# A hybrid decoder layer on one core: a new order of the opening, new places for gate and up's outputs, and the last tiles of W_o by halves in turn

## The chip, the cores and the metric

The kernel runs on one core of one Trainium2 chip. The metric is the device time of one execution in microseconds (us). The profile shows one execution, taken by the hardware profiler. Engines are named as the profile names them: PE is TensorE's matrix multiplication and PEld its loading of weights, DVE is VectorE, ACT is ScalarE, POOL is GpSimd, SP is SyncE, which only issues DMA transfers. "SPq" and "POOLq" mark what an engine's sequencer does.

## The reference

One layer of a decoder (width 1024) over a prompt of 2048 tokens and, beside it, over 8 decode tokens that come with a window of keys and values and with a state. All arrays are float32. What is computed, cut to its core:

```python
def finish(x, o_attn, o_gla, r_gla, gla_norm_g, w_o, ffn_norm_g, w_gate, w_up, w_down):
    ...
    h = x + jnp.concatenate([o_attn.astype(x.dtype), g], axis=-1) @ w_o
    z = rmsnorm(h, ffn_norm_g)
    return h + (jax.nn.silu(z @ w_gate) * (z @ w_up)) @ w_down

def reference(...):
    ...
    q_a, k_a, v_a, q_g, k_g, v_g, r_g, log_a = project(rmsnorm(xp, attn_norm_g[l]), *proj_w)
    o_a = prompt_window_attention(q_a, k_a, v_a, rel_bias, attn_sinks[l])
    ...
    o_g, s_p = gla_chunked(q_g, k_g, v_g, log_a, s0)
    xp = finish(xp, o_a, o_g, r_g, *ffn_w)
```

`project` is one product with `w_in` (1024 x 2320), followed by norms of each head. The attention is a sliding window of 128 keys with sinks and a relative bias; group B is gated linear attention (GLA). D_FF is 2816. For the decode tokens the window of keys and values moves on by one: 127 rows of each cache go to the outputs `k_win_sample` and `v_win_sample` as they are, and the new row behind them.

## The kernel before

**Precision.** Each float32 operand is split into a high and a low part (`split`, line 96: ScalarE casts the high part, VectorE subtracts it), and each product is three matmuls (`mm3`, line 107; lines 109 to 111 of the profile): high by high, high by low, low by high. So nearly each operand costs one instruction on ACT and one on DVE (lines 97 and 98 of the profile) before PE can use it.

**Order.** The tile framework orders the instructions of each engine with a planner that runs a simulated timeline over the whole program. The program's text sets priorities, not the order: an instruction without dependencies, such as a load, may be put far ahead of where it stands. `tc.issue_after(ins)` binds the instructions of a block that run on `ins`'s engine to come after `ins` in that engine's order. Nearly all DMA transfers are issued by SP in one order; an issue that waits holds up those behind it. Some are issued by POOL, on its own queue.

**Stage A (lines 149 to 596): projection and attention, block by block of 128 tokens.** `front(b)` loads a block of x, normalises it, transposes it on PE (line 144) and splits it. `project(b)` multiplies it with WA (q, k, v and the low-rank gate's columns, 784 wide), `project_r(b)` with WR (512 wide), `attend(b)` computes the attention and stores it in `mix_d[b]`. WA and WR are loaded and split once, at the opening, by `staged_split` (line 178); every second call of it, if the piece is large enough, takes the piece as one load of 1024 columns, the others in loads of 512. `make_bias` (line 523) multiplies a one-hot table with the bias table on PE (line 538), stores the result (`ext`) in DRAM (line 541), loads it back shifted for each row (`rev`, line 548) and flips it on PE (line 550) into `bias`, which `attend` needs. `nTdec` is a zeroed tile (line 85) which the decode tokens' `norm_T` fills later. The decode tokens' part of the stage is a generator that is advanced once in each block. At b == 3 stands a block (lines 581 to 592) with loads for the next stage (gg, w2, bT) and two copies from cache to output inside DRAM.

**Stage B (lines 628 to 1000)** is the gated linear attention; it adds to `mix_d`.

**Stage M (lines 1077 to 1225): W_o, residual, norm, and the operands of gate and up.** The 16 tiles of 128 tokens, and then the 8 decode tokens as tile NB, go through `load_tile`, `product` (two halves `dh` of W_o's columns, 24 matmuls each at 512 columns, or 16 for the decode tokens) and `after`, which calls `normalise` for the tile before and, for every second tile, `operands`. gate and up are computed with Strassen's scheme in the form with seven products: `operands` forms the seven sums of z's four quarters (b11, b21, b12, b22), splits them and stores them in `zc_d` by POOL's queue. Three buffers (`hlp`) hold what is being stored; the last four of the last tile go into the memory of the two `mix` tiles.

**Gate and up (lines 1283 to 1366).** The tokens go in two halves `sb` of 1024, and for each half in 11 pairs `fp` of weight columns. `pair` runs the seven products in the order P1, P6, P2, P7, P5, P4, P3 for gate and up. Each product needs one z operand in SBUF (`zc`, 2 MB each, loaded at line 1361) and one split weight unit (`whl`). P1 is copied out of PSUM by ACT into `p1` (line 1256), and P2 goes on accumulating in the same bank. The outputs of the products live in 14 tiles of 516 columns (`out`, line 1231), two for each of seven names.

**Memory.** The SBUF is filled from both ends. Stage M's tiles on the right lie, from the highest address down, as: z operands 0 and 1, W_o's two halves, the two mix tiles, three store buffers, gBf with z, and lowest b0 to b3 with zd. In gate and up, z operands 2 and 3 take the place of W_o's first half, 4 and 5 that of the second half, 6 that of the mix tiles, and the 14 output tiles lie over the rest, lowest first in the order in which their names first occur within a pool. So each of these loads and first writes waits until the last reader of what lay there is done.

**Down (lines 1370 to 1475)** multiplies with w_down in the same scheme and adds to h; it uses the same `out` tiles.

Of the kernel before, what the change touches and what calls it, by code (L numbers as in the profile page):

```python
# [53 lines left out]
def hymba_kernel(ctx: ExitStack, tc: tile.TileContext, I, O, X=None, phases=3):  # L54
# [94 lines left out]
    with ExitStack() as ph:  # L149
# [15 lines left out]

        gB = early.tile([P, D], F32, name="gB")
# [9 lines left out]
        staged = [0]  # L176
# [16 lines left out]
        def load_wq(k, nk):  # L193
            staged_split(WA[:, 0, k:k + nk, 0:512], WA[:, 1, k:k + nk, 0:512], w_in[:, k:k + nk, 0:512], 512)

        def load_wkv(k):
            staged_split(WA[:, 0, k:k + 4, 512:768], WA[:, 1, k:k + 4, 512:768], w_in[:, k:k + 4, 512:768], 256)
# [4 lines left out]
        def load_wr(k):  # L202
            staged_split(WR[:, 0, k:k + 2], WR[:, 1, k:k + 2], w_in[:, k:k + 2, 1792:2304], 512)
# [157 lines left out]
        def attend(b):  # L361
# [62 lines left out]
            nc.sync.dma_start(mix_d[b][:, 0:4, :], o.rearrange("p (c t) -> p c t", c=4))  # L424
# [98 lines left out]
        def make_bias():  # L523


            with tc.tile_pool(name="a_ext", bufs=1) as ep:
# [17 lines left out]
                nc.sync.dma_start(dbias_d[:, 0:1], ext[:, P - 1:P])  # L544

# [21 lines left out]
        project(1)  # L567
        project_r(0)
        project_r(1)
        dec = decode_a()  # L570
        for b in range(NB):
# [6 lines left out]
            attend(b)  # L578
            if b >= 1:
                next(dec, None)  # L580
            if b == 3:
                nc.sync.dma_start(gg, I["gla_norm_g"].rearrange("o d -> d o"))
                w2 = pc.tile([16, 256], F32, name="w2")
                nc.sync.dma_start(w2, I["w_gla_gate2"][0])
                split(w3[0:16], w3[64:80], w2)
                nc.vector.tensor_copy(w3[32:48], w3[0:16].bitcast(F32))
                for p in range(2):
                    nc.sync.dma_start(bT[:, p:p + 1], I["b_gla_gate"][0:1, p * P:(p + 1) * P].rearrange("o d -> d o"))
                nc.gpsimd.tensor_scalar(nbT, bT, -1.0, None, ALU.mult)
                for nm_, cache in (("k_win_sample", "cache_k"), ("v_win_sample", "cache_v")):  # L590
                    nc.sync.dma_start(O[nm_][0, :, 0:P - 1].rearrange("n t h d -> n t (h d)"),
                                      I[cache][0, :, 1:P].rearrange("n t h d -> n t (h d)"))
# [473 lines left out]

    def load_w(w, fp):
        raws = []
        for kh in range(2):
            wr = craw.tile([P, 1024], F32, tag="raw", name="wrg").rearrange("p (k n) -> p k n", k=4)  # L1070
            nc.sync.dma_start(wr, w[kh * 512:(kh + 1) * 512, fp * 256:(fp + 1) * 256].rearrange("(k p) n -> p k n", p=P))
# [5 lines left out]
    with ExitStack() as ph:  # L1077
# [6 lines left out]
        zp = pool(ph, "m_z", 1, side="right")  # L1084
        bp = pool(ph, "m_b", 1, side="right")
# [42 lines left out]
        def product(ti, mt, h):  # L1128
            n = P if ti < NB else ND
            for dh in range(2):  # L1130
# [8 lines left out]
                add_h(h, n, dh, ps)  # L1139
            if ti < NB:  # L1140
# [3 lines left out]
            return h  # L1144
# [66 lines left out]
        for i, ti in enumerate(tiles):  # L1211
# [5 lines left out]
            hs[ti] = product(ti, *now)  # L1217
            if ti < NB and i:
                after(tiles[i - 1])
# [63 lines left out]
    with ExitStack() as ph:  # L1283
# [74 lines left out]
        for sb in range(2):  # L1358
            zc = {name: ztile(q, f"z{q}") for q, name in enumerate(PRODS)}
            for q, name in enumerate(PRODS):  # L1360
                nc.sync.dma_start(zc[name][:, :, :, 0:512].bitcast(F32), zc_d[sb][q])
# [3 lines left out]
            for fp in range(NP):  # L1365
                pair(sb, fp, zc)

# [161 lines left out]
```

## Time and profile before

| | us |
|---|---|
| median of three runs | 2242.85 |
| lowest and highest of them | 2240.05, 2245.52 |
| the profiled execution | 2241.9 |
| its span, first to last instruction | 2239.8 |
| PE busy in it | 2184.7 |

The granted clock of TensorE is 0.994 on the mean of the span. The busy share of PE, the granted clock and the share of the DMA engines in 40 equal slices of 56 us, as tenths:

```profile
PE   7999998999999999899999999999999999999997
PEclk9999999999999999999999999999999999999999
DMA  7323325445535898842333376445352698779776
```

Stage A takes the first 6 or 7 slices, stage B lasts until the 13th, stage M fills slices 13 to 16, gate and up 17 to 32, down the rest. A row of a timeline reads: start in us, duration in us, engine, line, operation, tiles (written <- read), shape, count, and in brackets how long the engine sat idle before it and what ended that.

### The profile page before, as it was taken

Reading aid. Unit: us, or ns where it says so; the run is one execution under the profiler, and the core shown is the slowest. Engines: PE = TensorE matmul, PEld = TensorE weight load, DVE = VectorE, ACT = ScalarE, POOL = GpSimd, SP = SyncE. Lnnn points to the kernel's source line nnn. Section 1 sums busy time; section 2 is a strip of 40 time slices with the busy share of each in tenths; the row PEclk is TensorE's granted clock in tenths of the full one; section 3 lists DMA queues with packets and bytes.
Section 4 is the critical chain, followed back from the end, with each engine's and each line's share of the span. In section 5 each row is a group of like instructions: output and inputs, shape, how many; then the busy total and the mean of one; then the engine's idle time right before and its main releaser. Section 6 shows DMA issues by size and latency. Waiting matters only on the chain.

```text
span 2239.8 us, 34849 instructions
## 1 busy us (share of the span) xinstructions
PE 2184.7 (98%) x12573; PEld 1883.0 (84%) x12573; DVE 1579.5 (71%) x3129; ACT 982.0 (44%) x2249; POOL 686.7 (31%) x788
## 2 busy tenths in 40 slices
PE   7999998999999999899999999999999999999997
PEld 6788887888897887688888889999999978787886
DVE  7788888677866667666666667777776645657486
ACT  6656766565655344323333233334333324334342
POOL 2555665574665233111111111110111122222222
PEclk9999999999999999999999999999999999999999
DMA  7323325445535898842333376445352698779776
GB/s 228 110 77 119 119 77 183 125 152 167 175 116 199 298 350 272 316 131 82 113 95 107 105 266 216 149 127 165 101 187 86 220 285 188 184 170 243 167 195 236
DMA packets 218060, 386.35 MB, mean 172 GB/s; under 512 B 16440, under 2 KB 129872, under 8 KB 214800
## 3 DMA queue, kind: packets, MB, share of 16 engines
q1 hardware_dynamic: 180400, 279.48, 37.7%
q0 software_dynamic: 37488, 104.65, 18.1%
q8 instruction: 99, 1.62, 0.3%
q14 instruction: 73, 0.60, 0.1%
HBM read 221.84 MB, written 163.30 MB: 172 GB/s over the span
## 4 chain that ended last, share of the span: by engine, by line
PE 55%; issue 18%; DVE 10%; POOL 6%; ACT 4%; DMA 3%; SPq 0%; POOLq 0%; DVEq 0%; ACTq 0%
PE ps_b L110 5%; PE ps_b L109 5%; PE ps_b L111 5%; POOL h_d L1457 4%; PE ps_c L110 4%; PE ps_c L109 4%; PE ps_c L111 4%; PE ps_a L110 4%; PE ps_a L111 4%; PE ps_a L109 4%; PE ps_wo L111 2%; PE ps_wo L109 2%; PE ps_wo L110 2%; ACT S L394 1%; PE ps_v L109 1%
## 5 line engine op out<-in xcount | busy, mean ns | idle before, releaser
L110 PE MATMUL ps_b<-z,whl 128*128 128x258 f32 (+1 forms) x792 | 253.4, 320 | 0.0
L109 PE MATMUL ps_b<-z,whl 128*128 128x258 f32 (+1 forms) x792 | 253.0, 320 | 0.0
L111 PE MATMUL ps_b<-z,whl 128*128 128x258 f32 (+1 forms) x792 | 252.1, 318 | 0.0
L97 ACT CAST dm<-mr 128x384 fp32r<-128x384 f32 (+1 forms) x224 | 107.8, 488 | 201.9 <-PE ps_b L111 102.4
L109 PE MATMUL ps_a<-z,whl 128*128 128x258 f32 (+1 forms) x528 | 169.8, 322 | 5.1 <-ACT gp L1256 4.4
L109 PE MATMUL ps_c<-z,whl 128*128 128x258 f32 (+1 forms) x528 | 169.4, 321 | 2.1 <-DMA z<-zc_d_P 2.1
L111 PE MATMUL ps_a<-z,whl 128*128 128x258 f32 (+1 forms) x528 | 169.6, 321 | 0.5 <-DVE whl L98 0.5
L110 PE MATMUL ps_a<-z,whl 128*128 128x258 f32 (+1 forms) x528 | 169.7, 321 | 0.0
L110 PE MATMUL ps_c<-z,whl 128*128 128x258 f32 (+1 forms) x528 | 169.6, 321 | 0.0
L111 PE MATMUL ps_c<-z,whl 128*128 128x258 f32 (+1 forms) x528 | 169.5, 321 | 0.0
L98 DVE TENSOR_TENSOR dm<-mr,dm 128x384 fp32r<-128x384 f32 (+1 forms) x224 | 115.2, 519 | 64.3 <-ACT dm L97 64.1
L111 PEld LDWEIGHTS ps_b<-z,whl 128*128 128x128 f32 x792 | 148.8, 188 | 11.9
L109 PEld LDWEIGHTS ps_b<-z,whl 128*128 128x128 f32 x792 | 148.9, 188 | 11.8
L110 PEld LDWEIGHTS ps_b<-z,whl 128*128 128x128 f32 x792 | 148.8, 188 | 11.8
L97 ACT CAST whl<-wrg 128x512 fp32r<-128x512 f32 x132 | 81.6, 619 | 162.1 <-PE ps_b L111 76.8
L1356 POOL DMA_DIRECT2D md_d<-m x22 | 15.6, 710 | 356.7 <-DVE m L1315 356.7
L1023 DVE TENSOR_TENSOR gu<-ps_c,gu 128x512 f32<-128x512 f32 (+1 forms) x130 | 77.9, 599 | 53.0 <-PE ps_c L111 52.3
L98 DVE TENSOR_TENSOR whl<-wrg,whl 128x512 fp32r<-128x512 f32 x132 | 90.7, 688 | 33.8 <-ACT whl L97 33.7
L849 POOL TENSOR_TENSOR bd<-E,qTb 64x256 f32<-64x256 f32 x112 | 101.5, 906 | 41.4 <-ACT E L837 26.6
L109 PEld LDWEIGHTS ps_a<-z,whl 128*128 128x128 f32 x528 | 100.1, 190 | 13.9 <-ACT gp L1256 4.8
L97 ACT CAST whl<-sy 128x512 fp32r<-128x512 f32 x88 | 54.5, 619 | 125.0 <-PE ps_b L111 70.9
L109 PEld LDWEIGHTS ps_c<-z,whl 128*128 128x128 f32 x528 | 100.1, 190 | 10.6 <-issue 2.5
(424 smaller groups left out, 6681.0 us busy)
## 6 DMA issues: line engine op xcount, KB each, us to landing
mr<-md_d SPq DMA_DIRECT2D x24, 1344.0 KB
zc_d_P<-zhl POOLq DMA_DIRECT2D x56, 512.0 KB, 6.8
z<-zc_d_P SPq DMA_DIRECT2D x14, 2048.0 KB
wrg<-in_w_gate_dram SPq DMA_DIRECT2D x44, 512.0 KB
wrg<-in_w_up_dram SPq DMA_DIRECT2D x44, 512.0 KB
nT_d<-nT SPq DMA_DIRECT2D x16, 1024.0 KB
zT<-nT_d SPq DMA_DIRECT2D x8, 2048.0 KB
h_d<-gu POOLq DMA_DIRECT2D x48, 256.0 KB, 5.4
```

What stands on the lines that cost most here:

```text
L97: nc.scalar.copy(h, src)
L98: (eng or nc.vector).tensor_tensor(l, src, h.bitcast(F32), ALU.subtract)
L109: nc.tensor.matmul(ps, lh, rh, start=start, stop=False, skip_group_check=more)
L110: nc.tensor.matmul(ps, lh, rl, start=False, stop=False, skip_group_check=more)
L111: nc.tensor.matmul(ps, ll, rh, start=False, stop=stop, skip_group_check=more)
L394: nc.scalar.activation(St[:, c], St[:, c], AF.Exp, bias=nm[:, h:h + 1], accum_out=den[:, h:h + 1])
L849: nc.gpsimd.tensor_tensor(bv[rows, h], E5[rows, :, :, 1], qv[rows, :, :, 1], ALU.mult)
L1023: nc.vector.tensor_tensor(out, a, b, ALU.add)
L1356: nc.gpsimd.dma_start(md_d[sb][g][:, :, q, fp - GROUPS[g][0], :], src.rearrange("p (m t) -> p m t", m=4))
L1457: nc.gpsimd.dma_start(h_d[ti][:, cols], c, accum_op=ALU.add)
```

## The change

- **Opening.** 30 matmuls on the zeroed `nTdec` come first on PE, and ten transposes of tile 0 after `front(0)`, all into a PSUM tile that nobody reads. `front(1)` stands ahead of the last four of the q weights; the low-rank columns are loaded after k and v's. Which pieces come as one load is given by position. `make_bias` is a generator: its first part (to the store of `ext`) stands where it stood, its second after `project(1)`.
- **The block at b == 3.** The loads of gg, w2 and bT are bound behind the store of `attend(3)`; the two cache copies move to gate and up, behind the weight loads of the third pair of the first half.
- **Stage M.** `product` yields after each half of W_o; for the last tile (15) and the decode tokens the halves are run in turn: 15 first half, NB first half, 15 second half, NB second half, and then tile 11's `after`. A pool of 128 columns that nobody uses lies where zd made room, and zd now lies in mdec's memory.
- **Gate and up.** The 14 output tiles are placed one by one in three pools: m11, gu3, uu3 (first of each) and m11's second in the lowest; gp1, up1, gu2, uu2 (first of each) in the next; the others above. The seventh z operand of the first half is loaded by POOL's queue.

```diff
+        zeros = nTdec.rearrange("p k t -> p (k t)")
+        ps_warm = aux.tile([P, 512], F32, tag="aux", name="ps_warm")
+        for i in range(30):
+            nc.tensor.matmul(ps_warm[:, :320], zeros[:, 0:P], zeros, start=True, stop=True)
...
-        def staged_split(hi, lo, src, width):
+        def staged_split(hi, lo, src, width, whole=False):
...
-            staged[0] += 1
-            if staged[0] % 2 == 0 and nk * width > 512:
+            if whole:
...
         front(0)
+        for i in range(10):
+            nc.tensor.transpose(ps_warm[:, :P], xt0[:, 0:P], ident)
         load_wq(0, 1)
         load_wq(1, 1)
-        for k in range(2, KD, 2):
+        load_wq(2, 2)
+        front(1)
+        for k in range(4, KD, 2):
             load_wq(k, 2)
-        front(1)
-        load_lr()
         load_wkv(0)
         load_wkv(4)
+        load_lr()
         load_gains()
-        make_bias()
+        turn = make_bias()
+        next(turn)
         for k in range(0, KD, 2):
             load_wr(k)
         project(0)
         project(1)
+        next(turn, None)
         project_r(0)
...
-            attend(b)
+            stored = attend(b)
...
             if b == 3:
...
+                with tc.issue_after(stored.ins):
+                    nc.sync.dma_start(gg, I["gla_norm_g"].rearrange("o d -> d o"))
+                    nc.sync.dma_start(w2, I["w_gla_gate2"][0])
...
-                for nm_, cache in (("k_win_sample", "cache_k"), ("v_win_sample", "cache_v")):
-                    nc.sync.dma_start(O[nm_][0, :, 0:P - 1].rearrange("n t h d -> n t (h d)"),
-                                      I[cache][0, :, 1:P].rearrange("n t h d -> n t (h d)"))
...
+        pool(ph, "m_gap", 1, side="right").tile([P, 128], F32, name="gap")
         bp = pool(ph, "m_b", 1, side="right")
...
                 add_h(h, n, dh, ps)
+                yield
...
-                d = bp.tile([P, 8, 4, 4], F32, name="zd")
+                d = mdec.rearrange("p f n -> p (f n)")[:, 0:128].rearrange("p (q k t) -> p q k t", q=8, k=4)
...
-            hs[ti] = product(ti, *now)
-            if ti < NB and i:
-                after(tiles[i - 1])
+            hs[ti] = now[1]
+            if i < len(tiles) - 2:
+                for _ in product(ti, *now):
+                    pass
+                if i:
+                    after(tiles[i - 1])
+            elif ti < NB:
+                last = product(ti, *now)
+            else:
+                both = last, product(ti, *now)
+                for _ in range(3):
+                    for p in both:
+                        next(p, None)
+                after(tiles[-3])
...
-    cy1, cy2 = pool(ctx, "c_out1", 2), pool(ctx, "c_out2", 2)
+    cys = [pool(ctx, f"c_out{i}", 1) for i in range(3)]
+    PLACE = {"m110": 0, "m111": 0, "gu30": 0, "uu30": 0, "gp10": 1, "up10": 1, "gu20": 1, "uu20": 1}
+    turns = {}
 
     def out(tag, name):
-        return (cy2 if tag in ("gu3", "uu2", "uu3") else cy1).tile([P, 516], F32, tag=tag, name=name)
+        n = turns[tag] = turns.get(tag, -1) + 1
+        tag += str(n % 2)
+        return cys[PLACE.get(tag, 2)].tile([P, 516], F32, tag=tag, name=name)
...
-                nc.sync.dma_start(zc[name][:, :, :, 0:512].bitcast(F32), zc_d[sb][q])
+                (nc.gpsimd if (sb, q) == (0, 6) else nc.sync).dma_start(zc[name][:, :, :, 0:512].bitcast(F32), zc_d[sb][q])
...
                 pair(sb, fp, zc)
+                if sb == 0 and fp == 2:
+                    with tc.issue_after(loaded[0].ins):
+                        for nm_, cache in (("k_win_sample", "cache_k"), ("v_win_sample", "cache_v")):
+                            nc.sync.dma_start(O[nm_][0, :, 0:P - 1].rearrange("n t h d -> n t (h d)"),
+                                              I[cache][0, :, 1:P].rearrange("n t h d -> n t (h d)"))
```

`loaded[0]` is the last weight load that `load_w` issued.

More of the change, by code (lines that the diff above doesn't have):

```diff
@@ L174, in hymba_kernel @@
         w_in = I["w_in"][0].rearrange("(k p) n -> p k n", p=P)
-        staged = [0]
-        def staged_split(hi, lo, src, width):
+        def staged_split(hi, lo, src, width, whole=False):
             nk = src.shape[1]
-            staged[0] += 1
-            if staged[0] % 2 == 0 and nk * width > 512:
+            if whole:
                 wr = wl.tile([P, D], F32, tag="pT", name="wr", bufs=3).rearrange("p (k n) -> p k n", n=width)
@@ L193, in load_wq @@
         def load_wq(k, nk):
-            staged_split(WA[:, 0, k:k + nk, 0:512], WA[:, 1, k:k + nk, 0:512], w_in[:, k:k + nk, 0:512], 512)
+            staged_split(WA[:, 0, k:k + nk, 0:512], WA[:, 1, k:k + nk, 0:512], w_in[:, k:k + nk, 0:512], 512, k == 4)
         def load_wkv(k):
-            staged_split(WA[:, 0, k:k + 4, 512:768], WA[:, 1, k:k + 4, 512:768], w_in[:, k:k + 4, 512:768], 256)
+            staged_split(WA[:, 0, k:k + 4, 512:768], WA[:, 1, k:k + 4, 512:768], w_in[:, k:k + 4, 512:768], 256, True)
         def load_lr():
@@ L202, in load_wr @@
         def load_wr(k):
-            staged_split(WR[:, 0, k:k + 2], WR[:, 1, k:k + 2], w_in[:, k:k + 2, 1792:2304], 512)
+            staged_split(WR[:, 0, k:k + 2], WR[:, 1, k:k + 2], w_in[:, k:k + 2, 1792:2304], 512, k % 4 == 2)
         gq = pc.tile([P, 1], F32, name="gq")
@@ L423, in attend @@
                 nc.vector.tensor_tensor(o[rh], po[rh], ol[rh], ALU.add)
-            nc.sync.dma_start(mix_d[b][:, 0:4, :], o.rearrange("p (c t) -> p c t", c=4))
+            return nc.sync.dma_start(mix_d[b][:, 0:4, :], o.rearrange("p (c t) -> p c t", c=4))
         def decode_a():
@@ L581, in hymba_kernel @@
             if b == 3:
-                nc.sync.dma_start(gg, I["gla_norm_g"].rearrange("o d -> d o"))
                 w2 = pc.tile([16, 256], F32, name="w2")
[L584 to L589, printed above, removed]
-                for nm_, cache in (("k_win_sample", "cache_k"), ("v_win_sample", "cache_v")):
-                    nc.sync.dma_start(O[nm_][0, :, 0:P - 1].rearrange("n t h d -> n t (h d)"),
-                                      I[cache][0, :, 1:P].rearrange("n t h d -> n t (h d)"))
+                with tc.issue_after(stored.ins):
+                    nc.sync.dma_start(gg, I["gla_norm_g"].rearrange("o d -> d o"))
+                    nc.sync.dma_start(w2, I["w_gla_gate2"][0])
+                    split(w3[0:16], w3[64:80], w2)
+                    nc.vector.tensor_copy(w3[32:48], w3[0:16].bitcast(F32))
+                    for p in range(2):
+                        nc.sync.dma_start(bT[:, p:p + 1], I["b_gla_gate"][0:1, p * P:(p + 1) * P].rearrange("o d -> d o"))
+                    nc.gpsimd.tensor_scalar(nbT, bT, -1.0, None, ALU.mult)
         project_r(NB - 2)
@@ L1065, in sums_b @@
         yield b22
+    loaded = [None]
     def load_w(w, fp):
@@ L1070, in load_w @@
             wr = craw.tile([P, 1024], F32, tag="raw", name="wrg").rearrange("p (k n) -> p k n", k=4)
-            nc.sync.dma_start(wr, w[kh * 512:(kh + 1) * 512, fp * 256:(fp + 1) * 256].rearrange("(k p) n -> p k n", p=P))
+            loaded[0] = nc.sync.dma_start(wr, w[kh * 512:(kh + 1) * 512, fp * 256:(fp + 1) * 256].rearrange("(k p) n -> p k n", p=P))
             raws.append(wr)
@@ L1139, in product @@
                 add_h(h, n, dh, ps)
+                yield
             if ti < NB:
@@ L1143, in product @@
                 nc.gpsimd.dma_start(hdec_d, h[:n])
-            return h
         def normalise(ti, h, bs):
```

## The prediction

> **What bounds the kernel now.** I read the page's busy times first, then the waits of TensorE (PE) in the two stretches that the change touches, then the timelines of the queues there.
>
> ```profile
> PE 2184.7 (98%) x12573; PEld 1883.0 (84%) x12573; DVE 1579.5 (71%) x3129; ACT 982.0 (44%) x2249; POOL 686.7 (31%) x788
> ```
>
> TensorE is busy 2184.7 of 2239.8 us. The change takes no matmul of the computation away, so it can only win idle TensorE time (55.1 us in all) and time at the lower clock. Here are the PE waits of the first 150 us, and then those of 860 to 1000 us, where the W_o phase turns into the gate/up phase (columns: total, times, longest):
>
> ```profile
> PE ps_nT L144 <- DVE xt L139: 8.5, 2, 8.3
> PE ps_rev L550 <- DMA rev<-ext_d: 1.9, 1, 1.9
> PE ps_nT L144 <- DVE nTdec L98: 1.5, 1, 1.5
> PE ps_nT L144 <- DVE xtd L139: 1.1, 1, 1.1
> ```
>
> ```profile
> PE ps_a L109 <- ACT gp L1256: 4.4, 1, 4.4
> PE ps_c L109 <- DMA z<-zc_d_P: 2.1, 1, 2.1
> PE ps_a L109 <- ACT whl L97: 0.7, 1, 0.7
> PE ps_a L111 <- DVE whl L98: 0.5, 1, 0.5
> ```
>
> The 8.3 us are the first tile's load and norm, which the change does not shorten. What can go is the wait for rev (1.9), and the four at the turn (7.7). The waits at 91 to 97 us (1.5 and 1.1) belong to the decode tokens' norm, which is not edited.
>
> A wait costs more than itself, because the clock drops. The windows view (busy, PEclk, DMA share, GB/s) behind each wait:
>
> ```profile
> 46.00:51.00 5.00, 4.50 (x16) 0.66 0.22 75
> 914.00:918.00 4.00, 3.66 (x10) 0.57 1.03 394
> 927.00:932.00 5.00, 5.00 (x16) 0.66 1.06 383
> ```
>
> The loss is (1 - 0.66) x 5 = 1.7 us after rev, (1 - 0.57) x 4 = 1.7 after the wait for gp, and again 1.7 after that for z. The Trainium skill, "TensorE: Matmul & The Clock Gate", Part 1, says that the clock falls back only after an idle window of about 3.4 us. By that rule the gaps of 1.95 and 2.08 us would cost no clock, and the sum below would be 1.7 + 1.7 smaller before any part is discounted. The rows with 0.66 say otherwise here, so the measurement decides.
>
> **The opening.** The PE timeline of the start:
>
> ```profile
> 8.32 1.97 PE L144 MATMUL ps_nT<-ident,xt 128*128 128x128 f32 x8 [8.32 <-DVE xt L139]
> 10.18 0.80 PE L109 MATMUL ps_d<-WA,nT 128*128 128x512 f32 x1
> ...
> 13.18 0.39 PE L110 MATMUL ps_d<-WA,nT 128*128 128x512 f32 x1
> 13.40 0.39 PE L111 MATMUL ps_d<-WA,nT 128*128 128x512 f32 x1
> ...
> 17.48 1.07 PE L144 MATMUL ps_nT<-ident,xt 128*128 128x128 f32 x8 [0.22 <-DVE xt L139]
> ```
>
> Seven matmuls start between 10.18 and 13.18, 0.43 us apart; later ones are 0.23 apart (13.18 to 13.40). That is 3.0 against 7 x 0.23 = 1.6: 1.4 lost. The eight transposes take 1.97 against 1.07: 0.9 lost. PE is cold from 8.32 to 13.2, 4.9 us, although the clock column still reads 1.00 there. The 30 matmuls on zeros (320 columns) cost 0.43 x 320/512 = 0.27 us each cold, 0.14 warm. They need only nTdec's memset:
>
> ```profile
> 0.87 0.37 POOL L85 MEMSET nTdec<- 128x320 f32 x1
> ```
>
> From 1.24 on, 4.9 us hold 18 cold ones, and 12 warm ones take 1.7: they end at 7.8, before the 8.32 at which real work can start. If all stayed cold they would end at 9.3 and cost 1.0. Nothing else runs on PE then, so the cover is complete. The ten extra transposes on tile 0 are 10 x 1.07/8 = 1.3 us. They lie where PE otherwise waits for nT's split; uncovered they cost the 1.3.
>
> The gain of 2.3 is capped by the weights. The windows view (busy of PE, PEld, DVE, ACT, POOL, clock, DMA share, GB/s) and the DVE timeline:
>
> ```profile
> 10.00:20.00 10.00, 9.19 (x37) 6.55 (x35) 8.78 (x13) 8.18 (x15) 1.96 (x2) 1.00 0.99 286
> ```
>
> ```profile
> 12.14 2.43 DVE L98 TENSOR_TENSOR WA<-wr,WA 128x1024 fp32r<-128x1024 f32 x3
> ...
> 17.25 3.47 DVE L98 TENSOR_TENSOR WA<-wr,WA 128x1024 fp32r<-128x1024 f32 x4
> ```
>
> The DMA engines are full (0.99) and the k and v weights are split only by 20.7. A PE that is early must have other work: tile 1's q product, for which x of tile 1 and front(1) are moved ahead of the last q weights. That moves 0.5 MB of x in front of 1 MB of weights at 286 GB/s, 1.8 us on those. Bounds: -1.3 (transposes uncovered) to 2.3; I take **1.5**. That wkv(0) now comes in one piece instead of two, that lr comes after wkv, and that the other pieces are told by position are the same bytes: 0, hidden behind the full DMA engines.
>
> **The bias.** ScalarE's copy of ext, SP's queue in its order of issue, and PE at the wait:
>
> ```profile
> 26.67 0.36 ACT L540 COPY ext<-ps_ext 8x256 f32<-8x256 f32 x1
> ```
>
> ```profile
> 26.63 0.65 SPq L582 DMA_DIRECT2D gg<-in_gla_norm_g_dram  x1
> ...
> 31.53 0.81 SPq L591 DMA_DIRECT2D out_k_win_sample_dram<-in_cache_k_dram  x1
> ...
> 33.48 3.78 SPq L591 DMA_DIRECT2D out_v_win_sample_dram<-in_cache_v_dram  x1
> 37.36 0.60 SPq L541 DMA_DIRECT2D ext_d<-ext  x1
> ...
> 42.78 1.09 SPq L548 DMA_DIRECT2D rev<-ext_d  x2
> ```
>
> ```profile
> 46.51 1.46 PE L550 MATMUL ps_rev<-rev,flip 128*128 128x512 f32 x2 [1.95 <-DMA rev<-ext_d]
> ```
>
> ext is there at 27.0 but stored only at 37.36, since gg, w2, bT and the two cache copies (all from the block at b == 3) stand ahead of it in SP's order. The change ties the first three behind attend(3)'s store and takes the copies out of this phase. The quoted entries alone are 0.65 + 0.81 + 3.78 = 5.2 us of issue; PE needed rev 1.95 us earlier. The wait and its clock loss, 1.95 + 1.7 = 3.65, can go. The matmuls on rev also stand behind project(0) and project(1) now, which gives the load more time. What is late next is VectorE:
>
> ```profile
> 44.50:56.00 11.50, 9.55 (x45) 7.31 (x45) 9.43 (x25) 9.26 (x21) 6.20 (x8) 0.85 0.38 113
> ```
>
> It is busy 9.43 of 11.5 us, so part of the gap can return as a wait for the next norm or the scores. Bounds 0 to 3.65; I take **2.5**. A shifted plan can move the waits at 91 to 97 us, 1.5 + 1.1, either way: 0 in the sum, 2.6 kept at both ends.
>
> The cache copies go behind the third pair of gate/up, where SP pays 0.81 + 3.78 again ahead of later weight loads:
>
> ```profile
> 960.00:1000.00 40.00, 40.00 (x174) 32.35 (x173) 29.55 (x47) 12.28 (x21) 7.91 (x11) 1.00 0.39 125
> ```
>
> There DMA has room (0.39) and PE is never idle: cost 0, covered by the weights split ahead; without that cover up to 4.6. gg, w2 and bT are first needed in the next phase: 0.
>
> **The turn to gate/up.** First who held P2 up, from the timelines of ACT and DVE:
>
> ```profile
> 913.52 0.28 ACT L97 CAST zdec<-zd 128x112 fp32r<-128x112 f32 x1 [0.16 <-DVE zd L1020]
> 913.71 0.58 ACT L1256 COPY gp<-ps_a 128x512 f32<-128x512 f32 x1
> ```
>
> ```profile
> 901.06 1.27 DVE L1155 SCALAR_TENSOR_TENSOR zd<-h,rs_r,gBf 8x1024 f32<-8x1024 f32 x1
> ```
>
> P2 accumulates in P1's bank, so it waits until ACT has copied P1 to gp, and ACT does that at 913.71, behind the last work on the b tiles and zd. By the sizes in the code gp's first tile (2064 bytes, third of the old pool) lies over b2 and b3, which the last tile's operands read until about then. In the new order it lies over the gap and gBf, whose last reader is the row at 901.06, done at 902.3; up, gu2 and uu2 lie over gBf and z, gu3, uu3 and m11 over the b tiles, and these are written one to three products later. zd in mdec's memory leaves nothing of it under the out tiles. So gp can be copied some 10 us before P2 needs it, and 4.4 + 1.7 = **6.1** goes. VectorE, which is busy until 914, is late next: P7 needs its two additions, but P2 for gate and up gives it 24 x 0.23 = 5.5 us first.
>
> Then the wait for z (P5's operand). SP's queue, W_o for the decode tokens on PE, and the windows:
>
> ```profile
> 893.19 21.18 SPq L1361 DMA_DIRECT2D z<-zc_d_P  x4
> 914.48 11.89 SPq L1071 DMA_DIRECT2D wrg<-in_w_gate_dram  x2
> ...
> 930.39 2.03 SPq L1361 DMA_DIRECT2D z<-zc_d_P  x1
> ```
>
> ```profile
> 889.20 7.67 PE L1137 MATMUL ps_wo<-WO,mixdec 128*40 128x512 f32 x32
> ```
>
> ```profile
> 881.00:893.00 12.00, 12.00 (x57) 8.68 (x56) 12.00 (x21) 5.33 (x10) 4.69 (x6) 1.00 0.77 226
> 893.00:905.00 12.00, 12.00 (x57) 8.75 (x56) 10.03 (x17) 5.19 (x10) 4.33 (x7) 1.00 0.99 333
> ```
>
> The z loads start when W_o's first half is free, at 893.19. By halves in turn, the last tile's second half (24 x 0.23 = 5.5 us) and tile 11's transposes come after it: free about 6.5 us earlier. But in 881 to 893 the DMA engines are already 0.77 busy, so the head start carries 0.23 x 6.5 = 1.5 us of full transfer, and the rest shares with the stores of the operands. The fifth load no longer stands behind four weight loads on SP; on POOL's queue it waits for the last operand stores, whose space it takes, and behind it there wait only stores of products, with 14 out tiles of room. The gain is the wait and its clock, 2.1 + 1.7 = 3.8, and the two waits for whl, 1.2, at best; 0 at worst, as everything is at full DMA. I take half of the 3.8, **1.9**. The price of the halves: the last tile's product ends later by half of the 7.67, 3.8 us, and so do its norm and its operands; they are read a whole half later, so 0, but the fifth load starts later by that.
>
> The Trainium skill, "DMA: Bandwidth & Descriptors", section "Queues, rings and completion order", says that each DMA engine serves the queues that have work in turn, packet by packet. By that rule a load on POOL's queue doesn't add rate but takes it from SP's loads in flight. The landing times of the stores, in the next fence, agree with such sharing.
>
> **Sum.** 1.5 + 2.5 + 6.1 + 1.9 = 12.0. The profiled execution took 2241.9 us (span 2239.8); less 12.0 is 2229.9. The median of the three runs is 2242.85, 0.95 above it: **2231**.
>
> **Rivals.** *DMA-bound turn* (0.20). The wait for gp goes and comes back at z, because all bytes between 893 and 932 move at full rate: of the turn only 1.5 remain; with 1.5 + 2.5 from the opening that is 5.5: 2237. For it: DMA 1.03 and 1.06 in the windows above. Against it: z for P2 and P7 come first, and P5 needs only the third load.
>
> *The opening gives nothing* (0.15): zeros don't raise the clock, or the weights (0.99) swallow it, and VectorE takes rev's place. Only 8.0 is left: 2235.
>
> *Slower: stores starved at the turn* (0.07). The operands' stores, POOL line 1193, min/median/max us:
>
> ```profile
> DMA to landing us min/median/max: 3.9/6.9/10.2
> ```
>
> There are three buffers for them; if z's early loads push the landings from 3.9 to 10.2, ACT waits 6.3 us more for a buffer, twice, and VectorE, which works in order, holds the weight splits back behind it. With 1.7 of clock each that is 16, against 12 won: 2243 + 4 = 2247. It decides if the stores in flight at 887 land after about 895.
>
> *All of it and more* (0.08): 2.3 + 3.65 + 7.7 + 3.4 + 2.6 = 19.7: 2223.
>
> **Chances.** The forecast has 0.50. A measurement of this kernel tells about 0.2%, 4.5 us, from no change: faster means under 2238.4. Faster: forecast, best case and weak opening, 0.73, and a quarter of the DMA case, which lies only 1.4 under that line: 0.78. Same: the rest of the DMA case, 0.15. Slower: the stores, 0.07. The range goes from near the best case, 2224, to the DMA case with the 2.6 of a shifted plan lost, 2240; outside it lie the slower case and most of the best one, 0.15.
>
> **What would show it.** Right: matmuls 0.23 apart from the first on tile 0; rev off PE's list of waits and ext_d stored before 30; ACT's copy to gp before 905; no wait for z over 1 us. Wrong: a wait for z or whl of 4 us at the turn; PE under 0.9 clock in 44 to 56; new waits at the end of the attention phase from another plan.

## The result and the profile after

The changed kernel takes 2232.28 us (median of 7 runs, 2228.61 to 2236.14), the kernel before in the same comparison 2242.85 (2240.05 to 2247.53). The ratio is 0.995, with a 95% interval of 0.994 to 0.9959: 10.6 us are gone. The profiled execution took 2235.04 us, its span is 2233.1, so it is one of the longer ones, 2.8 over the median. The two profiled spans, 2239.8 and 2233.1, differ by 6.7.

Busy times on the page of after, to be held against those of before:

```profile
PE 2185.7 (98%) x12613; PEld 1889.3 (85%) x12613; DVE 1576.0 (71%) x3128; ACT 981.0 (44%) x2248; POOL 694.6 (31%) x789
```

PE has forty instructions more (30 on zeros, ten transposes). What went is idle time, so the waits come next. The longest of PE's waits in 0 to 150 us after the change (total, times, longest):

```profile
PE ps_nT L144 <- DVE nTdec L98: 3.1, 1, 3.1
PE ps_d L109 <- ACT qs L310: 2.8, 1, 2.8
PE ps_d L109 <- ACT nT L97: 2.2, 1, 2.2
PE po L421 <- DVE o L426: 1.7, 1, 1.7
```

The wait for rev is off the list, but new ones of the same size stand on it, for ACT (qs, nT) above all. At the turn to gate and up, 870 to 1000 us, all four waits of before are replaced by one:

```profile
PE ps_b L109 <- DMA z<-zc_d_P: 4.0, 1, 4.0
```

and the windows of after around it (busy of PE, PEld, DVE, ACT, POOL, clock, DMA share, GB/s) show why and what it costs:

```profile
893.00:905.00 12.00, 12.00 (x58) 8.70 (x57) 8.57 (x14) 5.05 (x9) 4.33 (x5) 1.00 1.03 383
905.00:917.00 12.00, 12.00 (x62) 9.66 (x61) 10.52 (x23) 6.90 (x13) 4.06 (x5) 1.00 1.04 401
917.00:930.00 13.00, 10.38 (x45) 8.08 (x43) 7.27 (x15) 4.49 (x8) 2.67 (x4) 1.00 1.03 392
...
931.30:937.00 5.70, 5.66 (x14) 4.49 (x15) 3.44 (x6) 1.15 (x2) 0.71 (x1) 0.51 0.83 264
```

For 37 us on end the DMA engines are full at 383 to 401 GB/s. PE runs without a gap until 927, then waits for an operand of z, and comes back at half clock.

The last thing to look at is the end of the program. The last POOL row of before and of after, each under its span:

```profile
core 0 of [0], span 2239.8 us
start us, us, engine line op out<-in xcount [idle before <-releaser]
2230.57 0.54 POOL L1452 DMA_DIRECT2D out_y_prompt_dram<-hq  x1 [0.82 <-DVE hq L1023]
```

```profile
core 0 of [0], span 2233.1 us
start us, us, engine line op out<-in xcount [idle before <-releaser]
2227.96 0.54 POOL L1489 DMA_DIRECT2D out_y_prompt_dram<-hq  x1 [0.81 <-DVE hq L1031]
```

From the last store's issue to the end of the span it is 9.2 us before and 5.1 after. The code there is the same, and the store lands after 2.3 us in both. What takes longer is the longest of POOL's three closing DRAIN instructions, which begins with that issue and ends 0.8 us before the span does (count, shortest/median/longest in ns, first and last start; before, then after):

```profile
L1525 POOLq DRAIN  x3: 40/93/8438, 2230.5 to 2239.5; - x3
```

```profile
L1562 POOLq DRAIN  x3: 40/93/4399, 2227.9 to 2232.8; - x3
```

The prediction has no term for this.

### The profile page after: what moved, and what is told of

Read it like the earlier page. It is cut to its first block, busy times and chain, and to the rows that moved or that the text cites. A ratio compares the mean times of both kernels' runs of the same rounds, so it can differ in the third digit from the quotient of the medians.

```text
span 2233.1 us, 34909 instructions
## 1 busy us (share of the span) xinstructions
PE 2185.7 (98%) x12613; PEld 1889.3 (85%) x12613; DVE 1576.0 (71%) x3128; ACT 981.0 (44%) x2248; POOL 694.6 (31%) x789
## 4 chain that ended last, share of the span: by engine, by line
PE 76%; issue 7%; DVE 7%; DMA 5%; POOL 2%; ACT 2%; SPq 0%; POOLq 0%; DVEq 0%; ACTq 0%
PE ps_b L110 7%; PE ps_b L109 7%; PE ps_b L111 7%; PE ps_c L110 5%; PE ps_c L111 5%; PE ps_c L109 5%; PE ps_a L109 5%; PE ps_a L110 5%; PE ps_a L111 4%; PE ps_wo L111 3%; PE ps_wo L109 3%; PE ps_wo L110 3%; PE ps_d L109 3%; PE ps_d L110 3%; PE ps_d L111 3%
```

## The experiments

My theory before them: the gain is that of the turn, and the opening gives nothing. The rival: both parts give what the prediction says, and the turn less.

Each diff is against the changed kernel unless it says otherwise; every ratio is against the kernel before in the same comparison.

### The opening and the turn apart

The turn alone (only the diff's last part: halves, gap, places of the outputs, zd, seventh z load on POOL; the opening, the bias and the block at b == 3 as before):

```diff
-        zeros = nTdec.rearrange("p k t -> p (k t)")
...
-        turn = make_bias()
-        next(turn)
+        make_bias()
```

> Stages M and gate/up as after the change; the opening, the bias and the block at b == 3 (with the cache copies) as before it. After's trace has project_r(1) end at 51.39 us against 49.67 before, and the first W_o matmul 0.7 us later than before: the opening seems to have won nothing. Theory (the opening is worth nothing, the turn 4.2 us and more): as fast as the changed kernel within 2 us, a ratio to before of 0.995 to 0.997. Rival (the prediction's split: opening 4.0, turn 8.0): 8 us under before, slower than the changed kernel by 4, and a turn without the 4.0 us wait for z.

Measured: 2232.94 against 2244.23, ratio 0.9951 (0.9938 to 0.9964). PE's only wait at its turn is the 4.1 us for z.

The opening alone (zeros, order, bias, b == 3 and the cache copies; the turn as before):

```diff
-    cys = [pool(ctx, f"c_out{i}", 1) for i in range(3)]
+    cy1, cy2 = pool(ctx, "c_out1", 2), pool(ctx, "c_out2", 2)
...
-            hs[ti] = now[1]
+            hs[ti] = product(ti, *now)
```

> The opening, the bias and the block at b == 3 as after the change (the cache copies in gate/up); everything else as before it. Theory: 0 to 2 us to either side of before, ratio 0.999 to 1.001; the first tile's q product starts at 12.6 instead of 10.2 us, and stage B starts within 1 us of before. Rival (prediction): 4 us faster, ratio 0.998.

Measured: 2244.28, ratio 1.0001 (0.9991 to 1.0011). PE's waits at its turn, 860 to 1000 us, are those of before again:

```profile
PE ps_a L109 <- ACT gp L1266: 4.4, 1, 4.4
PE ps_a L109 <- ACT whl L97: 2.2, 1, 2.2
PE ps_c L109 <- DMA z<-zc_d_P: 1.4, 1, 1.4
```

Its profiled execution is its fastest of eleven (2239.66). There the attention ends at 401.7 instead of 406.6, where the theory said within 1 us, so a single profile would credit the opening with a gain that the eleven times don't have.

What follows: the whole measurable gain is in the part called the turn, and the opening with the bias is worth 0.0 ± 2.2 us (0.001 of 2244).

### Why the opening gives nothing

Two kernels that each undo one step of it. First, front(1) behind all q weights:

```diff
         load_wq(2, 2)
-        front(1)
         for k in range(4, KD, 2):
             load_wq(k, 2)
+        front(1)
```

> The changed kernel with front(1) behind all q weights again. Theory: ScalarE, which works in order, had the square of tile 1 in front of the cast of tile 0's transposes and waited for x of tile 1 until 10.88; with front(1) back the first matmul of tile 0 starts at about 9.6 us instead of 12.56, and project_r(1) ends 2 us or more earlier than 51.4. Whether that reaches the end is open, since stage A's lead was lost before the next stage: 0 to 3 us faster than the changed kernel. Rival (the weights' DMA holds the opening): the first matmul is earlier but project_r(1) ends at 51 as before.

Measured: 2230.35, ratio 0.9941 (0.9929 to 0.9953). Second, without the zeros and the ten transposes:

```diff
-        for i in range(30):
-            nc.tensor.matmul(ps_warm[:, :320], zeros[:, 0:P], zeros, start=True, stop=True)
...
-        for i in range(10):
-            nc.tensor.transpose(ps_warm[:, :P], xt0[:, 0:P], ident)
```

> The changed kernel without the 30 matmuls on zeros and without the ten extra transposes (neither result is read). Theory: PE is cold at 8.3 us again, the eight transposes take about 2.0 instead of 1.1 us and the first matmuls start 0.43 us apart, but the wait for ScalarE is the same; project_r(1) ends 1 to 2 us later, and the whole is 0 to 2 us slower than the changed kernel. Rival (the warm-up does nothing for the time): no difference.

Measured: 2230.77, ratio 0.9947 (0.9931 to 0.9962). By time neither can be told from the changed kernel's 0.995. The traces say what happens. PE at the start of after:

```profile
1.30 6.33 PE L170 MATMUL ps_warm<-nTdec 128*128 128x320 f32 x30 [1.30 <-POOL nTdec L85]
8.15 1.09 PE L144 MATMUL ps_nT<-ident,xt 128*128 128x128 f32 x8 [0.52 <-DVE xt L139]
9.08 1.26 PE L559 MATMUL ps_warm<-ident,xt 128*128 128x128 f32 x10
12.56 0.51 PE L109 MATMUL ps_d<-WA,nT 128*128 128x512 f32 x1 [2.22 <-ACT nT L97]
```

and the same in the kernel without zeros and extra transposes:

```profile
7.99 1.97 PE L144 MATMUL ps_nT<-ident,xt 128*128 128x128 f32 x8 [7.99 <-DVE xt L139]
10.06 0.80 PE L109 MATMUL ps_d<-WA,nT 128*128 128x512 f32 x1
```

The zeros do warm PE: eight transposes take 1.09 instead of 1.97, and the first q matmul 0.51 instead of 0.80. But it starts 2.5 us later. ACT's timeline in after says why:

```profile
8.90 1.30 ACT L97 CAST WA<-wr 128x512 fp32r<-128x512 f32 x2
10.88 1.06 ACT L136 ACTIVATE nT<-xt 128x1024 fp32r<-128x1024 f32 x1 [0.68 <-DMA xt<-in_x_prompt_dram]
11.85 0.19 ACT L136 ACTIVATION_READ_ACCUMULATOR nT<-xt 128x1 f32 x1
11.94 1.05 ACT L97 CAST nT<-ps_nT 128x512 fp32r<-128x512 f32 x2
```

ACT takes its instructions in the planner's order. It stands at the square of tile 1 (front(1), moved ahead), waits for tile 1's x, and only then casts nT of tile 0, which PE needs. In the kernel without the zeros and the extra transposes that cast begins at 9.43, although front(1) is early there too. With front(1) late but the zeros and transposes kept, the cast still begins only at 11.73, behind weight casts that stand ahead of it in that plan, and the first q matmul at 12.37 instead of the expected 9.6. So the late cast goes with the warm-up and not with front(1); by which step of the planner, no run shows.

At 20.38 PE waits once more, 2.8 us for ACT's qs, and comes back at half clock, which lasts to 28.9 (a window of after; columns as above):

```profile
23.00:29.00 6.00, 5.86 (x14) 4.61 (x15) 2.24 (x5) 1.53 (x5) 1.06 (x1) 0.51 1.03 323
```

The kernel without the warm-up waits 1.3 us for qs, and its clock stays full. The second tile's product for r ends at 49.67 in before, at 51.39 in after, at 49.40 with front(1) late (2 us earlier than in after, as the theory had it), and at 45.69 without the warm-up, where the theory expected it later than in after. All eight profiles with the warm-up have it between 48.52 and 51.39. So at this place the warm-up costs more than it saves. By time the two kernels are nevertheless the same within what these runs tell apart: 2230.77 against 2232.28.

### The bias alone

The kernel before with the bias part only, to see whether the opening's order eats its gain (diff against before):

```diff
-        make_bias()
+        turn = make_bias()
+        next(turn)
...
         project(1)
+        next(turn, None)
```

with the block at b == 3 and the cache copies as in the change.

> The kernel before with the bias part alone: make_bias in two pieces, the block at b == 3 bound behind attend(3), the cache copies in gate and up; the opening's order and the turn as before, no zeros. Theory (the bias part does win its wait and clock, and the opening's new order eats it): the wait of 1.9 for rev is gone, the second tile's r product ends 2 to 3.5 us before the 49.67 of the kernel before, and the time is 0.9985 to 0.999 of it. Rival (an engine that PE waits for later, ACT or VectorE in the attention phase, takes the gain back): r's second product is early, the first W_o matmul within 1 us of 683.23, and the time is 1.000.

Measured: 2256.99, ratio 1.0059 (1.0046 to 1.0071): slower by 13, which neither theory expected. The first half of the theory holds: the second tile's product for r ends at 46.12 instead of 49.67, 3.55 us earlier, the size that the prediction worked out for the wait and its clock (two other profiles with the old bias part have it at 47.26 and 49.31, so the gain is 1.1 to 3.6). But the next projection, that of the third tile, ends at 65.13 against 64.13 before: the gain is lost within 20 us. New waits for DVE stand in PE's list of the first 150 us:

```profile
PE ps_s L378 <- DVE rf_t L129: 1.4, 1, 1.4
PE ps_nT L144 <- DVE qT L339: 1.2, 1, 1.2
PE ps_s L378 <- DVE mx L387: 1.1, 1, 1.1
```

At the end of the attention the kernel looks 4.6 us ahead all the same (402.0 against 406.6). It isn't: this plan has 23 matmuls of stage B's products with its weights WV behind that mark which before has ahead of it, 0.23 us each, 5.3 us in all. So it is about level there, and what is lost is lost in later stages whose code it does not touch. The profiled execution, its fastest of five, has a span 10.1 us longer than before's. Stage B (end of the attention to the first W_o matmul) takes 289.3 us against 276.6. Of these 12.7 us, 6.2 are moved work: the 23 matmuls and eight others of 0.11 us that before runs behind the first W_o matmul. The other 6.5 are lost. PE waits eight times for POOL where before waits once (1.0 us), and behind one of these waits, of 1.9 us, it runs at half clock for 6.8 us, which costs 3.4:

```profile
PE ps_l L856 <- POOL bd L851: 5.9, 8, 1.9
```

The old turn takes 94.9 us against 91.5, with one wait of 12.3 us for z and full DMA engines:

```profile
PE ps_c L109 <- DMA z<-zc_d_P: 12.3, 1, 12.3
```

```profile
917.00:929.50 12.50, 0.17 (x4) 0.11 (x3) 11.05 (x26) 5.49 (x10) 5.14 (x6) 0.57 1.04 397
```

(the waits of 860 to 1000 us, and a window). The planner orders the whole program anew when its beginning changes, and this order is a worse one. So the parts of this change don't add up: opening and bias together are 1.0001, the bias alone is 1.0059.

### What the turn's gain is made of

Without the halves (tile 15 whole, then `after`, then the decode tokens):

```diff
-            if i < len(tiles) - 2:
-                for _ in product(ti, *now):
-                    pass
-                if i:
-                    after(tiles[i - 1])
-            elif ti < NB:
-                last = product(ti, *now)
...
+            for _ in product(ti, *now):
+                pass
+            if ti < NB and i:
+                after(tiles[i - 1])
```

> Everything of the change, but the halves of W_o are not run in turn: tile 15 whole, tile 14's rest, then the decode tokens. Theory (the turn is bound by the DMA engines, 383 to 400 GB/s from 893 on): z's first loads start some 5 us later, at a time at which the engines were only 0.77 busy, so the wait for the fifth product's operand is 2 to 4 us longer than the 4.0 of the changed kernel, and the time is 0.996 to 0.997 of the kernel before. Rival (the halves are worth nothing, the out places alone make the gain): the wait stays at 4.0 and the time is 0.995.

Measured: 2237.89, ratio 0.9971 (0.9959 to 0.9983), so by time the halves are worth 4.7 us of the changed kernel's gain (0.0021 of 2244), or 2.7 by the second comparison of the changed kernel, 0.9959, which stands further down; the intervals leave either value uncertain by 3 to 4 us. The theory's mechanism is not seen: the waits for z are 4.5 us against 4.0, not 2 to 4 longer. The profiled run is the fastest of ten (2232.93) and has three waits at the turn, 5.7 us in all, where after has one. None of them is followed by half clock, and the turn takes 86.4 us there, no more than with the halves. So what the halves are worth is in the times alone.

With the output tiles in the two old pools:

```diff
-    cys = [pool(ctx, f"c_out{i}", 1) for i in range(3)]
+    cy1, cy2 = pool(ctx, "c_out1", 2), pool(ctx, "c_out2", 2)
```

> Everything of the change, but the 14 output tiles lie in the two old pools. Theory (gp's place holds the second product up): PE waits again 4 to 9 us for ACT's copy to gp, since the last tile's operands now end later by half of the decode tokens' product; the wait for z at the fifth product shrinks by as much, as z has had that time to land. So the sum of the waits between 890 and 940 is 4 to 9 against 4.0, and the time is 0.995 to 0.998 of the kernel before. Rival (the two waits are independent): the gp wait comes on top of the 4.0 for z, 8 to 13 together, and the gain of the change is gone: 0.998 to 1.001.

Measured: 2236.91, ratio 0.9967 (0.9954 to 0.9979). ACT's copy to gp and PE's waits, 860 to 1000 us, in this kernel:

```profile
L1282 ACT COPY gp<-ps_a x2: 579/583/587, 915.9 to 936.0; 128x512 f32<-128x512 f32 x2
```

```profile
PE ps_c L109 <- DMA z<-zc_d_P: 6.5, 1, 6.5
PE ps_b L109 <- issue: 2.0, 1, 2.0
```

(The first row's columns: count, shortest/median/longest in ns, first and last start.) The copy to gp is late again, at 915.9 (before 913.7, after 908.1). It isn't named as the wait, because the planner has put the fifth product, for which z lands at 916.2, ahead of the second one: the copy's lateness is hidden behind the z wait. So the theory named the wrong wait, and its cause is seen only in the late copy. The sum of the waits, 8.5, lies in its range and in the rival's, the time in its range alone.

With the seventh z load on SP's queue, as before:

```diff
-                (nc.gpsimd if (sb, q) == (0, 6) else nc.sync).dma_start(zc[name][:, :, :, 0:512].bitcast(F32), zc_d[sb][q])
+                nc.sync.dma_start(zc[name][:, :, :, 0:512].bitcast(F32), zc_d[sb][q])
```

> The changed kernel with the seventh z operand of the first half loaded by SP's queue, as before, instead of by POOL's. Theory (its queue doesn't matter, because on POOL it is issued only at 942, behind POOL's own waits, and is needed last): the same time within 0.1%, 0.995, and the wait of 4.0 at the fifth product as it was. Rival (on SP it blocks the weight loads behind it until the last operand stores have freed its place): a new wait for whl or for the weights of 2 to 5 us between 925 and 960, 0.996 to 0.998.

Measured: 2236.61, ratio 0.9967 (0.9954 to 0.9979). The theory gave 0.995 and fell. The rival gave the time, but not by its mechanism: PE's only wait at the turn is that of after, 4.1 us for z, with no new wait for weights behind it. The difference is at the end of the program:

```profile
core 0 of [0], span 2234.5 us
start us, us, engine line op out<-in xcount [idle before <-releaser]
2225.36 0.54 POOL L1489 DMA_DIRECT2D out_y_prompt_dram<-hq  x1 [0.82 <-DVE hq L1031]
```

It is 9.1 us from the last store to the end, 9.2 in before, and POOL's DRAIN is 8.44 again. It is the same to 0.01 us in every profile of a kernel with the seventh load on SP (four), and 4.40 in every one with it on POOL and the stores there too (seven). The 4.04 agree with the ratios: 0.0017 of 2244 is 3.8 (1.8 by the second comparison of the changed kernel).

With the last tile's operand stores on SP's queue, behind z's loads, instead of on POOL's beside them:

```diff
-                nc.gpsimd.dma_start(zc_d[sb][q][:, :, :, mt * P:mt * P + P], hl.bitcast(F32))
+                (nc.sync if (sb, mt) == (1, 3) else nc.gpsimd).dma_start(zc_d[sb][q][:, :, :, mt * P:mt * P + P], hl.bitcast(F32))
```

> The changed kernel with the last tile's seven operand stores on SP's queue, behind the z loads that stand there, instead of on POOL's queue beside them. Theory (sharing: the stores, which land 7 to 9.5 us after their issue, take rate from the z loads that PE waits for): the fifth operand lands earlier, the wait of 4.0 at z goes or falls under 1, and the time is 2 to 4 us below the changed kernel's, 0.993 to 0.994 of the kernel before. Rival (all bytes are needed anyway and the engines are full): the wait only moves to a later operand or weight, 2 to 4 us elsewhere between 925 and 960, and the time stays at 0.995.

Measured: 2228.41, ratio 0.9931 (0.9918 to 0.9944), as the theory had it. PE's only wait in 860 to 1000, and then the windows that in after held the wait and the slow clock:

```profile
PE ps_b L109 <- ACT b L1176: 1.6, 1, 1.6
```

```profile
917.00:930.00 13.00, 13.00 (x58) 10.52 (x57) 10.34 (x20) 5.62 (x10) 1.48 (x2) 1.00 1.10 351
930.00:945.00 15.00, 15.00 (x67) 12.11 (x66) 10.20 (x17) 5.55 (x10) 1.63 (x2) 1.00 0.92 308
```

Seven stores of 512 KB compete with z's loads in after; at 390 GB/s these 3.67 MB are 9.4 us of full transfer. Their reader is the second half of gate and up, hundreds of us later. Behind z in the same queue they cost PE no wait. The Trainium skill, "DMA: Bandwidth & Descriptors", section "Queues, rings and completion order", says that a DMA engine serves the queues with work in turn, packet by packet; this run agrees in so far as taking the stores out of the second queue took away PE's 4.0. That the turns are packets, it does not show.

### Together

The turn alone with the stores on SP (against the kernel with the turn alone):

```diff
-                nc.gpsimd.dma_start(zc_d[sb][q][:, :, :, mt * P:mt * P + P], hl.bitcast(F32))
+                (nc.sync if (sb, mt) == (1, 3) else nc.gpsimd).dma_start(zc_d[sb][q][:, :, :, mt * P:mt * P + P], hl.bitcast(F32))
```

> The kernel before with the turn's part alone (halves, places, zd, seventh load on POOL) and the last tile's operand stores on SP's queue. Theory (nothing of the opening is needed, and the stores on SP are worth 4 us in any company): 0.9930 to 0.9935 of the kernel before, with waits of PE under 2 us between 890 and 960. Rival (the gain of the stores on SP was the opening's, by another plan): 0.995.

Measured: 2229.32, ratio 0.9936 (0.9923 to 0.995), beside the theory's range by 0.0001; PE's only wait at the turn is 0.3. With the bias part added:

```diff
-        make_bias()
+        turn = make_bias()
+        next(turn)
...
+        next(turn, None)
```

> The same as the run before with the bias part too: the changed kernel less the zeros, the extra transposes and the new order of the opening, with the last tile's operand stores on SP's queue. Theory (the bias part wins its own 2 to 3.5 us where the opening's order does not take them): 0.9915 to 0.992. Rival (the attention phase takes them back): the same as the run before, 0.993.

Measured: 2227.52, ratio 0.994 (0.9926 to 0.9953): the bias part adds nothing that these runs can tell, as its rival said (the medians differ by 1.8 us, the ratios the other way). The end of the attention is 7.5 us earlier than in before, but the same 23 matmuls stand behind it, so the lead is 2.2. Stage B takes 286.5 against 276.6, 6.2 of it moved work as with the bias alone, and gives the lead back.

The changed kernel again, on the chip of the bias alone and of these two:

> The changed kernel again, on the chip of the three runs before, to compare with. If the chip doesn't matter: 0.995, and the same 4.0 us wait for z at the fifth product.

Measured: 2232.46, ratio 0.9959 (0.9946 to 0.9971), with the wait for z at 3.0. Three kernels with the stores on SP stand at 0.9931, 0.9936 and 0.994, the changed kernel and its turn alone at 0.995, 0.9959 and 0.9951. The stores on SP beat both kernels: 2228.41 is the best of these with the change otherwise whole, some 4 us under it. Whether another order of the opening would help on top is below what these runs tell apart.

## Why the prediction was right, point by point

2231 was forecast and 2232.28 measured. But the sum, 1.5 + 2.5 + 6.1 + 1.9, is right only as a sum, and that was luck: the opening's two terms, 4.0, were near nothing, and a term of 4.0 was missing. The profiles by stage (us; worked out from PE's rows: the turn is the time from the last W_o matmul to the 336th one of gate and up):

| kernel | last W_o matmul ends | turn | POOL's DRAIN | span |
|---|---|---|---|---|
| before | 896.9 | 91.5 | 8.44 | 2239.8 |
| opening alone | 892.9 | 92.2 | 8.44 | 2237.4 |
| old places | 894.1 | 92.1 | 4.40 | 2233.9 |
| after | 897.0 | 87.2 | 4.40 | 2233.1 |
| after again | 896.2 | 83.8 | 4.40 | 2229.7 |
| turn alone | 894.5 | 86.5 | 4.40 | 2232.2 |
| seventh load on SP | 893.9 | 86.4 | 8.44 | 2234.5 |
| stores on SP | 895.0 | 82.4 | 3.99 | 2227.2 |
| turn alone, stores on SP | 898.0 | 81.5 | 4.00 | 2227.5 |

The first column of times moves by up to 4 us between kernels with the same opening (opening alone, old places, after, again, seventh load, stores on SP), so one profile says little on the opening; the times say more.

- **The opening, 1.5: failed.** The step was that a warm PE with tile 1's work at hand is ahead. The transposes and the first matmuls are warm, as foreseen. But the prediction looked at the weights and DVE for what is late next, and it was ACT's order: front(1) or weight casts before nT's cast, and qs after it. PE waits for ACT 2.2 and 2.8 us there, and the clock falls to half behind the second wait. With the warm-up the second tile's r ends at 48.5 to 51.4, without it at 45.7. Moved and added work counts on every engine; ACT was left out. In time, the rival *The opening gives nothing* is what happened, though not by its conditions: the zeros do warm PE, and ACT is late, not the weights or DVE.
- **The bias, 2.5: the mechanism right, the gain not kept.** ext_d is stored at 27.72 and PE's first flip of rev comes at 44.40 without a wait. In the changed kernel the opening's late start eats what this wins. Alone, the part wins the 3.55 at the place; then come waits for DVE in the next tiles, which take it back, and a replanned stage B and turn lose some 10 us more. The prediction named DVE as the next late engine and still kept two thirds of the gain, and it held no price for a new plan of later stages beyond the 2.6 in its range.
- **The wait for gp, 6.1: held in kind.** It is gone with the new places and the late copy is back with the old. ACT copies at 908.1, not before 905: PE runs P6 first and P1 only from 903.25 on, so the copy could not begin before about 906.
- **The wait for z, 1.9: failed.** The condition named as wrong, a wait for z of 4 us at the turn, came true: 4.0 us, and 2.8 of clock, (1 - 0.51) x 5.7. It moved from P5 to P4, the product behind it in the order. Here the rival *DMA-bound turn* was the better picture: all operand bytes go at full rate. Its price was too high, since the turn still wins: 91.5 and 92.2 with the old one, 83.8 to 87.2 in six kernels with the new one and the stores on POOL, on the mean 86.2. That is 5.7 against 8.0 forecast for both terms.
- **The seventh load on POOL's queue: costed at nothing, worth 4.0.** The prediction looked for what waits behind it on POOL at the turn, and found rightly that nothing does. The effect is at the program's end.
- **The cache copies in gate and up: 0, right.** From the 336th to the 1848th matmul of gate and up takes 351.30 us in all the profiles, with and without them.

So, as an estimate from the profiles, the 10.6 us are 4.0 at the end and about 5.7 at the turn; the rest, about 1, is the opening or chance. Of the slower rival, stores starved, nothing is seen: in the stretch of the prediction's row, 860 to 925, they land after 4.1 to 9.5 us, against 3.9 to 10.2 before, with the same median.

```profile
DMA to landing us min/median/max: 4.1/6.9/9.5
```

## What to carry to other kernels

At a change of phase, list all transfers in flight by who needs them first; a store whose reader is far away belongs in the same queue behind the urgent loads, not in a second queue beside them. When work is added or moved ahead, follow it in the order of each engine, the one for casts too: a step that waits there for its load holds up the one that PE needs. Where a planner orders the whole program, an edit at the start can cost some 10 us in stages that it doesn't touch, so compare the stages that weren't edited before crediting a gain to the edit. Before comparing two plans at a mark such as the end of a stage, count the matmuls that lie ahead of it: here 5.3 of 7.5 us were work put off.

## What the runs showed of the hardware that was not expected

**The closing DRAIN of POOL goes with its DMA traffic.** With 354 transfers issued by POOL it is 8.44 us (four kernels), with 355 it is 4.40 (seven), with 348 it is 3.99, 4.00 and 3.18. It repeats to 0.01 us in kernels that differ elsewhere. The last store has landed 2.3 us after its issue in each case, so the DRAIN goes on for 6.1 us after that in before and 2.1 in after. It is not the count alone (348 gives two values), and what sets it stays open; no run varied it by itself.

**The clock after a gap.** Windows behind the wait for z in after again (3.0 us) and behind one of 2.4 without the halves, against 0.51 behind the 4.0 us in after:

```profile
929.60:935.00 5.40, 5.35 (x23) 4.43 (x24) 3.65 (x6) 1.16 (x2) 0.67 (x1) 1.00 0.94 304
```

```profile
922.90:928.00 5.10, 5.01 (x22) 4.11 (x23) 0.69 (x1) 0.63 (x1) 0.00 (x0) 1.00 1.05 388
```

Both gaps leave the clock at 1.00. The prediction took the rows of 0.66 behind gaps of 1.95 and 2.08 as a reason to price every wait with 1.7 of clock. The two here agree with the Trainium skill, "TensorE: Matmul & The Clock Gate", Part 1, which lets the clock fall only after an idle window of about 3.4 us; those of before don't, since a gap of 2 us holds no such window wherever it begins. So gaps of like length have gone both ways here.

The traces' clock records show why. In each execution the stretches at half clock begin whole multiples of 3.41 us apart (in before at 47.10, 94.89, 367.96, 914.09 and 927.74), so they lie on a grid. First the grid's window that holds the gap of 2.08 in before, and the window behind it; then the two windows that share the gap of 3.0 in after again, and the two that share the gap of 2.4 without the halves:

```profile
924.33:927.74 3.41, 1.33 (x7) 1.09 (x7) 0.00 (x0) 0.62 (x1) 0.00 (x0) 1.00 1.05 393
927.74:931.15 3.41, 3.41 (x10) 2.65 (x9) 0.00 (x0) 0.00 (x0) 0.00 (x0) 0.50 1.06 390
```

```profile
924.47:927.88 3.41, 2.17 (x10) 1.42 (x8) 0.10 (x1) 0.00 (x0) 0.00 (x0) 1.00 1.03 394
927.88:931.29 3.41, 1.64 (x7) 1.42 (x8) 0.09 (x1) 0.01 (x1) 0.00 (x0) 1.00 1.06 365
```

```profile
918.12:921.53 3.41, 2.45 (x11) 1.66 (x9) 1.99 (x4) 1.00 (x2) 0.00 (x0) 1.00 1.04 398
921.53:924.94 3.41, 1.95 (x9) 1.63 (x10) 0.48 (x1) 0.00 (x0) 0.00 (x0) 1.00 1.04 399
```

In before PE is busy 1.33 of 3.41 us, 39% of a window, and the next window runs at half clock. In the other two the grid splits the gap, and no window has PE busy under 1.64, 48%. Cut in this way, the fourteen traces hold 8961 windows at full clock between 15 and 2220 us. All 35 with PE busy below 46% are followed by half clock, and so are 13 of the 58 between 46 and 61%, but none of the 8868 above. So in these runs a gap costs 1.7 us of clock, half of 3.41, once it fills more than about half of one window, and none where the grid splits it evenly enough. The grid lies differently in each execution (it is shifted by 1.3 us between after and after again), so for a gap of 2 to 3 us it is chance. A saved wait of that length should be priced with a clock loss of 0 to 1.7, not with 1.7.
